# Seven leading pairs, squares through PSUM and decay tables behind the values in a one-core encoder block

## The chip, the core and the metric

The kernel runs on one core of one Trainium2 chip, in one launch. The metric is the device time of that launch in microseconds. Three runs of the kernel before gave 1798.32, 1795.58 and 1797.25 us, median 1797.25.

## What is computed

One layer on 1024 tokens of width 1024, with 16 meta tokens put ahead, all in float32. The mixer normalises the input and multiplies it by one wide weight (`proj = u @ w_in`). The columns of the product feed two branches and their gates:

```python
rq, rk, rv, rg, a_cq, a_ckv, a_kr, a_gret, a_gmla = split(u @ w_in)
y_ret = group_norm(forward_retention(rq, rk, rv) + backward_retention(rq, rk, rv))
y_ret = (silu(rg) * y_ret) @ w_ret_out
y_mla = attention(q(rmsnorm(a_cq)), k(rmsnorm(a_ckv)), v(rmsnorm(a_ckv)), rope(a_kr)) @ w_mla_out
h = h + (sigmoid(a_gret) * y_ret + sigmoid(a_gmla) * y_mla) @ w_o
h = h + (silu(u2 @ w_gate) * (u2 @ w_up)) @ w_down          # u2 = rmsnorm(h)
out = rmsnorm(h)                                            # meta rows dropped
```

The retention weighs its scores with powers of one decay per head and direction. The tables of these powers (128 x 128 per head, rows and columns of powers) are made in the kernel from 16 decay values.

## The kernel before, in words

Every float32 product is made of three matmuls on rounded parts: high by high, high by low, low by high. ScalarE casts the high part of a weight (L209, L153) and VectorE subtracts it to get the low part (L210, L154). A pair is two blocks of 128 output columns by two halves of 512 tokens. `seven` (L183) makes a pair with seven block products instead of eight, in the order of `NAMES` (L30): 11, t2, t3, n1, 21, t4, 22. A product is 12 matmuls with 512 columns (four blocks of the inner dimension, three matmuls each). The sums of weight blocks that t2, t3, n1 and 22 need are made by GpSimd (L191 to L193, L207). `seven_out` (L229) runs the products in order and combines them from PSUM on VectorE. `rest_out` (L300) runs only five products and takes the sum of "11" and "21" from a tile that was kept.

The kernel is written with tile pools. A planner with a time model orders the instructions of each engine: at each moment it takes the ready instruction that comes first in the program. Each engine then works its list in that order, so an instruction that waits holds back all that is behind it. Loads and stores are all issued by SyncE, in its own list.

Order of the mixer's first part:

1. Six pairs (`NP` = 6, L40: the four of `rg` and the first two of the gates) lead with the products "11" and "21" while the input is still being loaded (L345 to L394). Their copies are kept in the pool `hold` (L322), those of the gates in memory (`e_d`). Meanwhile VectorE and ScalarE build the seven input blocks (`second`, L364, and L408 to L418).
2. The rests of the four `rg` pairs (L419, L577, L579), and between them `squares` (L448): the input is loaded again, ScalarE squares each of 16 pieces, and GpSimd adds 14 of them up (L456).
3. Four pairs of values, `project_v` (L525). Each result is transposed on TensorE and copied by ScalarE (L534). After the first come `input_norm` (L458) and `decays` (L479), which makes all decay tables; after the others `finish_gates` (L513), six tiles each: load, scale, Silu or Sigmoid, store.
4. Rotary queries and keys (`project_rope`).
5. Retention, head by head (`core`, L620). Behind each head but the second stands a filler (L805 to L816), a projection that TensorE can do while the retention's long chain of small steps runs: the remaining gates (`project_gates`, seven products, and `rest_gates`, five), `project_q`, `project_key`, `project_kv`. The last two fillers, `project_kv` and a gate pair, stand between the first steps of `z_split` (L825), which splits the retention's result for the next product.
6. The retention's output product (`ret_out`), then attention, the output product and the FFN.

`latent_part` (L710) adds up squares of the latent columns, on GpSimd (L719).

Of the kernel before, what the change touches and what calls it, by code (L numbers as in the profile page):

```python
# [36 lines left out]

DQ, DG, DL = 3, 3, 4

NP = 6  # L40

O_AT = ((6, 1), (6, 2), (6, 3), (7, 0), (7, 1), (7, 2))

# [5 lines left out]
def build(nc, tc, A, out):  # L49
# [4 lines left out]
    def mk(pl, shape, tag, dt=F32):  # L54
        count[0] += 1
        name = f"{tag}_{count[0]}"
        n = int(np.prod(shape[1:]))
        if n % LINE == 0:
            return pl.tile(list(shape), dt, tag=tag, name=name)
        t = pl.tile([shape[0], -(-n // LINE) * LINE], dt, tag=tag, name=name)[:, :n]  # L60
        return t if len(shape) == 2 else t.rearrange("p (a b) -> p a b", b=shape[2])
# [4 lines left out]
    def sb(ctx, name, bufs=1, side=None, space=None):  # L66
        kw = {"reuse_waits": "tile"}
        if side:
            kw["side"] = side
        if space is not None:  # L70
            kw["space"] = space
            if space == DRAM:
                kw = {"space": space}
        return ctx.enter_context(tc.tile_pool(name=name, bufs=bufs, **kw))
# [73 lines left out]
    def slot(pl, dt=F32):  # L148
        return mk(pl, (P, 512), "slot", dt)
# [102 lines left out]
    with ExitStack() as c1:  # L252
# [65 lines left out]

        U = [{} for _ in range(4)]
        cc, a1 = ExitStack(), ExitStack()  # L320
        tb = sb(cc, "tables")
        hold = sb(a1, "hold", NP - 1)  # L322
        with ExitStack() as c2:
            xp, wf, wb = sb(c2, "x", 16), sb(c2, "wfirst", 2), sb(c2, "wfirst_r", 3)
# [108 lines left out]
            dve.tensor_add(t, ps[0:NM, lo : lo + n], t)  # L433
            return t

        dec = mk(tb, (P, 2 * H), "dec")
        kwf, kwb, kwm, gch = [mk(tb, (P, H), t) for t in ("kwf", "kwb", "kwm", "gch")]
        rt = sb(a1, "rope")
        cosf, sinf = mk(rt, (P, S), "cosf"), mk(rt, (P, S), "sinf")
        tm = mk(rt, (NM, 2, 64), "tm")  # L440
# [7 lines left out]
        def squares(c):  # L448
            for k in range(KT):
                t = slot(xl)  # L450
                load(t, A["xT"][k, :, c * 512 : c * 512 + 512])
                if k == 0:
                    act.square(ss[c], t)
                else:
                    act.square(t, t)
                    pool.tensor_add(ss[c], ss[c], t)  # L456

        def input_norm():  # L458
            t = slot(xl)[:, : KT * NM]
# [15 lines left out]
            for c in range(2):  # L475
                for t in (cosf, sinf):
                    dve.tensor_mul(t[:, c * 512 : c * 512 + 512], t[:, c * 512 : c * 512 + 512], rstd_b[:, c * 512 : c * 512 + 512])

        def decays():  # L479
            idx = slot(xl)  # L480
            load(idx, A["idx"][:, : 4 * P])
            idc = mk(rt, (P, 3), "idc")
            load(idc, A["idx"][:, 4 * P :])
            load(dec, A["dec"].broadcast_to([P, 2 * H]))
            act.activation(dec, dec, AF.Exp)
            dve.tensor_scalar(dec, dec, -1.0, None, ALU.mult)
            ip, im = idx[:, 0:P], idx[:, P : 2 * P]
            rowf, rowb = idx[:, 2 * P : 3 * P], idx[:, 3 * P : 4 * P]
            dts = [slot(xl) for _ in range(2)]
            for h in range(H):  # L490
                lf, lb = dec[:, h : h + 1], dec[:, H + h : H + h + 1]
                t = dts[h // 4][:, (h % 4) * P : (h % 4) * P + P]
                dve.tensor_scalar(t, ip, lf, None, ALU.mult)
                dve.scalar_tensor_tensor(t, im, lb, t, ALU.mult, ALU.add)
                act.activation(t, t, AF.Exp)
                store(t_d[h], t)
            tts = [slot(xl), slot(sr)]
            for h in range(H):
                hs = slice((h % 2) * 64, (h % 2) * 64 + 64)
                for t, row, o in ((tts[0], rowf, 0), (tts[1], rowb, H)):  # L500
                    c = slice((h // 2) * P, (h // 2) * P + P)
                    act.activation(t[hs, c], row[hs], AF.Exp, scale=dec[hs, o + h : o + h + 1])
            for p in range(4):
                for i in range(2):
                    store(t_d[8 + 4 * i + p], tts[i][:, p * P : p * P + P])
            for t, i, o, n in ((kwf, 0, 0, P), (kwb, 1, H, P), (kwm, 2, 0, NM)):
                dve.tensor_scalar(t[:n], dec[:n, o : o + H], idc[:n, i : i + 1], None, ALU.mult)
                act.activation(t[:n], t[:n], AF.Exp)
            act.activation(gch[0:64], dec[0:64, 0:H], AF.Exp, scale=float(P))
            act.activation(gch[64:128], dec[64:128, H : 2 * H], AF.Exp, scale=float(P))  # L510
# [11 lines left out]
        unfinished += [(g_d, 2 * j, "11", AF.Sigmoid) for j in range(NP - 4)]  # L522


        def project_v(j):  # L525
            ps = mk(pc, (P, 512), "mm")

            def post(name, t):
                g = side_copy(name, t)
                pt = mk(pc, (P, 512), "mm")  # L530
                for i in range(4):
                    pe.transpose(pt[:, i * P : i * P + P], g[:, i * P : i * P + P], ident)
                vv = slot(cr)
                act.copy(vv, pt)  # L534
                store(v_d[2 * j + int(name[0]) - 1, :, half(name)], vv)

            seven_out(seven(w7, win(4 + j), U, (ps, M1 | M2)), cr, post)
            t = meta_sum(ps, 0, 256)
            for h in range(2):
                store(vm_d[2 * j + h], t[:, h * P : h * P + P])  # L540
# [40 lines left out]
        for j in range(4):  # L581
            project_v(j)
            if j == 0:
                input_norm()
                decays()
            else:
                finish_gates(unfinished[6 * j - 6 : 6 * j])
        for j in range(2):
            project_rope(j, False)
            project_rope(j, True)  # L590
# [119 lines left out]
        def latent_part(t, c, dst, col, first):  # L710
            n = c.stop - c.start
            hi = slot(cr, F32R)[:, :n]
            act.mul(hi, t, col)
            if first:
                act.square(lss[:, c], t)
            else:
                q = slot(cr)[:, :n]
                act.square(q, t)
                pool.tensor_add(lss[:, c], lss[:, c], q)  # L719
            lo = slot(cr)[:, :n]  # L720
            dve.scalar_tensor_tensor(lo, t, col, f(hi), ALU.mult, ALU.subtract)
            store(dst[0][:, c], f(hi))
            store(dst[1][:, c], lo)
# [73 lines left out]
        def project_gates(i):  # L797
            seven_out(seven(w7, win(12 + i), U), cr, gate_post(g_d if i < 4 else s_d, 2 * (i % 4)))

        def rest_gates(i):  # L800
            e = slot(cr)
            load(e, e_d[i])
            rest_out([(seven(w7, win(12 + i), U), e, gate_post(g_d, 2 * i))], cr)

        gates = [lambda i=i: project_gates(i) for i in range(2, 8)]  # L805
        rests = [lambda i=i: rest_gates(i) for i in range(2)]
        fillers = gates[:4] + [rests[0], project_q, rests[1], gates[4], project_key, project_kv, gates[5]]
        for p in range(4):
            t = core_pair(p)
            for h in range(2):  # L810
# [111 lines left out]
    with ExitStack() as c1:  # L922
# [2 lines left out]
        vt = mk(vp, (P, NB + 1, H, P), "vt", F32R)  # L925
        pool.memset(f(vt)[0:48, NB], 0.0)
        ps_s = sb(c1, "ps_s", NS, space=PSUM)
        ps_t = sb(c1, "ps_t", NT, space=PSUM)
        ps_o = sb(c1, "ps_o", NO, space=PSUM)

        w2 = sb(c1, "att2", 2)
        w4 = sb(c1, "att4", 4)
# [510 lines left out]
```

## Time and profile before

| | |
|---|---|
| profiled execution | 1798.07 us |
| its span, first to last instruction | 1796.0 us |
| TensorE busy | 1720.9 us (96%) |
| VectorE busy | 1337.8 us (74%) |
| ScalarE busy | 855.0 us (48%) |
| GpSimd busy | 832.5 us (46%) |
| mean granted TensorE clock | 0.989 |
| memory traffic | 250 MB, mean 139 GB/s |

TensorE is busy nearly all the time, so what counts is where it is idle and where its clock is granted at half. Matmuls overlap, so the durations that the timeline gives for one are longer than the distance to the next; the distance is read from how many start in a stretch.

### The profile page before, as it was taken

The page shows a single profiled execution, that of the slowest core. Times are in us where ns is not written, and L with a number is a line of the kernel's source. Part 1 is how long each engine was busy: PE and PEld are TensorE (multiplying, and loading weights), DVE is VectorE, ACT ScalarE, POOL GpSimd, SP SyncE. Part 2 cuts the span into 40 slices and gives each one's busy share as a digit, 9 for nine tenths or more (in the row PEclk, how much of TensorE's full clock was granted, in tenths as well). Part 3 has the DMA queues.
Part 4 walks back from the last instruction along what each step waited for, and adds up shares of the span by engine and source line. Part 5 has one row for each costly group of instructions (what it writes and reads, how often), then busy time and mean ns, then how long its engine had stood idle before and what let it go on. Part 6 is the DMA issues. An engine that isn't in the chain of part 4 may idle for free.

```text
span 1796.0 us, 26421 instructions
## 1 busy us (share of the span) xinstructions
PE 1720.9 (96%) x8804; PEld 1439.7 (80%) x8804; DVE 1337.8 (74%) x2411; ACT 855.0 (48%) x1606; POOL 832.5 (46%) x654
## 2 busy tenths in 40 slices
PE   8889999999998898999999999899999999999997
PEld 6668777888887777899998888788888888777787
DVE  8755478887988857788879657866667666887966
ACT  7435466344424523678778345423233323543435
POOL 2722257676644421134232423666667666433422
PEclk9999999999999999999999999999999999999999
DMA  7745423556646785011112645233333333754422
GB/s 247 224 142 205 140 92 107 187 179 209 224 141 220 221 291 182 22 37 28 41 46 69 230 159 172 76 106 101 119 98 99 98 115 103 256 185 140 148 61 94
DMA packets 144570, 252.03 MB, mean 140 GB/s; under 512 B 18793, under 2 KB 36642, under 8 KB 144434
## 3 DMA queue, kind: packets, MB, share of 16 engines
q1 hardware_dynamic: 144434, 250.35, 42.6%
q8 instruction: 69, 1.13, 0.3%
q14 instruction: 67, 0.55, 0.1%
HBM read 173.89 MB, written 76.33 MB: 139 GB/s over the span
## 4 chain that ended last, share of the span: by engine, by line
PE 52%; DVE 5%; DMA 3%; ACT 2%; issue 2%; POOL 0%; SPq 0%; DVEq 0%; ACTq 0%; POOLq 0%
PE mm L217 29%; PE mm L137 3%; PE mm L138 3%; PE mm L139 3%; PE o L1027 3%; PE t L997 3%; DVE slot L154 1%; PE s L137 1%; PE s L138 1%; PE s L139 1%; DMA slot<-g_d 1%; DVE slot L210 1%; DMA slot<-f_d 1%; ACT pth L999 1%; PE o L137 1%
## 5 line engine op out<-in xcount | busy, mean ns | idle before, releaser
L217 PE MATMUL mm<-slot,slot 128*128 128x512 f32 x2604 | 596.1, 390 | 9.1 <-DVE slot L210 4.5
L217 PEld LDWEIGHTS mm<-slot,slot 128*128 128x128 f32 x2604 | 488.5, 188 | 115.5 <-DVE slot L210 7.5
L209 ACT CAST slot<-slot 128x512 fp32r<-128x512 f32 (+1 forms) x415 | 247.1, 598 | 464.4 <-PE mm L217 392.2
L210 DVE TENSOR_TENSOR slot<-slot,slot 128x512 fp32r<-128x512 f32 (+1 forms) x415 | 371.9, 897 | 90.4 <-ACT slot L209 81.4
L217 PE MATMUL mm<-ht,slot 128*128 128x512 f32 x648 | 219.7, 400 | 5.9 <-DVE slot L210 2.8
L217 PE MATMUL mm<-h,slot 128*128 128x512 f32 x552 | 190.9, 406 | 13.9 <-ACT slot L209 10.3
L191 POOL TENSOR_TENSOR slot<-slot,slot 128x512 f32<-128x512 f32 (+1 forms) x61 | 88.5, 1451 | 201.9 <-DMA slot<-in_w_u 48.3
L207 POOL TENSOR_TENSOR slot<-slot,slot 128x512 f32<-128x512 f32 (+1 forms) x61 | 87.9, 1442 | 182.2 <-DVE slot L210 170.1
L217 PEld LDWEIGHTS mm<-ht,slot 128*128 128x128 f32 x648 | 122.0, 190 | 34.5 <-ACT slot L209 5.0
L217 PEld LDWEIGHTS mm<-h,slot 128*128 128x128 f32 x552 | 104.3, 191 | 40.6 <-ACT slot L209 12.6
L154 DVE TENSOR_TENSOR slot<-slot,slot 128x512 fp32r<-128x512 f32 x135 | 117.0, 882 | 17.8 <-ACT slot L153 17.0
L217 PE MATMUL mm<-lt,slot 128*128 128x512 f32 x324 | 128.0, 395 | 0.0
L192 POOL TENSOR_TENSOR slot<-slot,slot 128x512 f32<-128x512 f32 (+1 forms) x61 | 83.4, 1367 | 76.0 <-DVE slot L210 70.7
L153 ACT CAST slot<-slot 128x512 fp32r<-128x512 f32 x135 | 82.1, 620 | 71.4 <-DMA slot<-f_d 27.2
L217 PE MATMUL mm<-l,slot 128*128 128x512 f32 x276 | 110.4, 400 | 0.0
L987 DVE TENSOR_SCALAR_CACHE_REDUCE pr<-s,sq_c 128x384 f32<-128x384 f32 (+1 forms) x192 | 103.2, 574 | 6.8 <-PE t L1005 5.4
L139 PE MATMUL mm<-slot,slot 128*128 128x512 f32 (+1 forms) x288 | 105.4, 366 | 0.0
L138 PE MATMUL mm<-slot,slot 128*128 128x512 f32 (+1 forms) x288 | 105.3, 366 | 0.0
L137 PE MATMUL mm<-slot,slot 128*128 128x512 f32 (+1 forms) x288 | 105.2, 367 | 0.0
L1000 DVE TENSOR_TENSOR ptl<-t,pth 128x512 fp32r<-128x512 f32 x128 | 85.8, 685 | 21.4 <-ACT pth L999 20.5
L193 POOL TENSOR_TENSOR slot<-slot,slot 128x512 f32<-128x512 f32 (+1 forms) x61 | 89.2, 1462 | 1.6
L999 ACT CAST pth<-t 128x512 fp32r<-128x512 f32 x128 | 71.9, 580 | 27.1 <-PE t L997 26.7
(360 smaller groups left out, 3460.1 us busy)
## 6 DMA issues: line engine op xcount, KB each, us to landing
slot<-in_w_in SPq DMA_DIRECT2D x104, 256.0 KB
f_d<-slot SPq DMA_DIRECT2D x71, 256.0 KB
slot<-f_d SPq DMA_DIRECT2D x71, 256.0 KB
slot<-in_xT SPq DMA_DIRECT2D x48, 256.0 KB
slot<-z_d SPq DMA_DIRECT2D x44, 256.0 KB
slot<-in_w_g SPq DMA_DIRECT2D x44, 256.0 KB
slot<-in_w_u SPq DMA_DIRECT2D x44, 256.0 KB
slot<-in_w_dq SPq DMA_DIRECT2D x48, 192.0 KB
```

Source lines behind the costliest of these rows:

```text
L137: pe.matmul(ps, sh, mh, start=start, stop=False)
L138: pe.matmul(ps, sh, ml, start=False, stop=False)
L139: pe.matmul(ps, sl, mh, start=False, stop=stop)
L154: dve.tensor_sub(lo, t, f(hi))
L191: pool.tensor_add(s1, a21, a22)
L193: pool.tensor_sub(a21, a21, a11)
L207: pool.tensor_sub(s2, s2, a12)
L209: act.copy(hi, side[b])
L210: dve.tensor_sub(low, side[b], f(hi))
L217: pe.matmul(ps, sw[:, ks], sx, start=begins and q == qs[0] and i == 0, stop=q == nq - 1 and i == 2, skip_group_check=True)
L987: dve.tensor_scalar(pr[:, c], ps[:, :n], sq_c[:, qb : qb + 1], None, ALU.mult, ALU.max, accum_out=mx[:, j : j + 1])
L999: act.copy(pt[0][d], tp)
```

## The change

`NP` goes from 6 to 7: a third gate pair (block 14 of `w_in`) leads with "11" and "21", and in the fillers it is a `rest_gates` of five products where it was a `project_gates` of seven. `hold` has six slots instead of five, `e_d` three pieces instead of two. The small decay tiles move from a pool of their own to `mf`. A square of the input goes to a PSUM tile, and VectorE adds it to the sum; the latent squares are added by VectorE too. `decays` is cut in three (the 128 x 128 tables, the rows, the columns), issued after the first, second and third values, and held on VectorE and ScalarE behind the last copy of those values. That copy is halved between VectorE and ScalarE. The gates are finished in strides of three instead of blocks of six (7, 6 and 6 tiles). The fillers have another order, with the new rest last. In the attention stage the pools of PSUM tiles `ps_o` and `ps_t` are opened in the other order.

```diff
-NP = 6
+NP = 7
...
-        tb = sb(cc, "tables")
...
-        dec = mk(tb, (P, 2 * H), "dec")
-        kwf, kwb, kwm, gch = [mk(tb, (P, H), t) for t in ("kwf", "kwb", "kwm", "gch")]
+        dec = mk(mf, (P, 2 * H), "dec")
+        kwf, kwb, kwm, gch = [mk(mf, (P, H), t) for t in ("kwf", "kwb", "kwm", "gch")]
...
-                    act.square(t, t)
-                    pool.tensor_add(ss[c], ss[c], t)
+                    sq = mk(pc, (P, 512), "mm")
+                    act.square(sq, t)
+                    dve.tensor_add(ss[c], sq, ss[c])
...
+        idx, idc = slot(xl), mk(rt, (P, 3), "idc")
+
         def decays():
-            idx = slot(xl)
             load(idx, A["idx"][:, : 4 * P])
-            idc = mk(rt, (P, 3), "idc")
...
+
+        def decay_rows():
+            rowf, rowb = idx[:, 2 * P : 3 * P], idx[:, 3 * P : 4 * P]
             tts = [slot(xl), slot(sr)]
...
+
+        def decay_columns():
             for t, i, o, n in ((kwf, 0, 0, P), (kwb, 1, H, P), (kwm, 2, 0, NM)):
...
-                act.copy(vv, pt)
+                ends.append((dve.tensor_scalar(vv[:, 0:256], pt[:, 0:256], 1.0, None, ALU.mult), act.copy(vv[:, 256:512], pt[:, 256:512])))
...
             if j == 0:
                 input_norm()
-                decays()
-            else:
-                finish_gates(unfinished[6 * j - 6 : 6 * j])
+            if j < 3:
+                with tc.issue_after(ends[-1][0].ins), tc.issue_after(ends[-1][1].ins):
+                    (decays, decay_rows, decay_columns)[j]()
+            if j:
+                finish_gates(unfinished[j - 1 :: 3])
...
-                pool.tensor_add(lss[:, c], lss[:, c], q)
+                dve.tensor_add(lss[:, c], lss[:, c], q)
...
-        gates = [lambda i=i: project_gates(i) for i in range(2, 8)]
-        rests = [lambda i=i: rest_gates(i) for i in range(2)]
-        fillers = gates[:4] + [rests[0], project_q, rests[1], gates[4], project_key, project_kv, gates[5]]
+        gates = [lambda i=i: project_gates(i) for i in range(NP - 4, 8)]
+        rests = [lambda i=i: rest_gates(i) for i in range(NP - 4)]
+        fillers = [gates[0], gates[1], gates[2], rests[0], project_q, gates[3], gates[4], rests[1], project_key, project_kv, rests[2]]
...
         ps_s = sb(c1, "ps_s", NS, space=PSUM)
+        ps_o = sb(c1, "ps_o", NO, space=PSUM)
         ps_t = sb(c1, "ps_t", NT, space=PSUM)
-        ps_o = sb(c1, "ps_o", NO, space=PSUM)
```

## Rows read from the trace of the kernel before

**Rows 1.** 50 us stretches: us; PE, PEld, DVE, ACT, POOL busy (instructions); clock; DMA; GB/s.

```profile
0.00:50.00 50.00, 39.05 (x153) 30.15 (x154) 41.66 (x57) 35.40 (x64) 14.38 (x22) 0.98 0.71 244
50.00:100.00 50.00, 39.40 (x158) 30.34 (x157) 34.95 (x55) 25.88 (x59) 35.30 (x23) 0.91 0.64 204
...
150.00:200.00 50.00, 49.02 (x277) 39.60 (x276) 32.44 (x48) 27.97 (x49) 11.91 (x8) 1.00 0.67 232
...
1300.00:1350.00 50.00, 50.00 (x223) 41.40 (x222) 34.56 (x42) 16.77 (x29) 34.34 (x24) 1.00 0.33 106
```

**Rows 2.** TensorE's timeline to 130 us: start, duration, instruction, idle before, its releaser.

```profile
43.60 0.50 PE L217 MATMUL mm<-ht,slot 128*128 128x512 f32 x1 [1.35 <-ACT slot L209]
...
47.20 0.50 PE L217 MATMUL mm<-hn,slot 128*128 128x512 f32 x1 [2.35 <-ACT slot L209]
...
48.87 1.22 PE L217 MATMUL mm<-ht,slot 128*128 128x512 f32 x2 [0.93 <-DVE slot L210]
...
75.44 0.73 PE L217 MATMUL mm<-h,slot 128*128 128x512 f32 x2 [0.67 <-DVE slot L210]
...
79.25 0.50 PE L217 MATMUL mm<-ht,slot 128*128 128x512 f32 x1 [1.25 <-ACT slot L209]
...
96.65 0.79 PE L217 MATMUL mm<-h,slot 128*128 128x512 f32 x1 [8.67 <-ACT slot L209]
```

**Rows 3.** The same columns as rows 1, in stretches of 5 us.

```profile
10.00:15.00 5.00, 5.00 (x21) 4.06 (x21) 3.63 (x6) 3.14 (x5) 0.00 (x0) 1.00 1.06 399
...
45.00:50.00 5.00, 1.87 (x5) 1.24 (x6) 5.00 (x10) 2.63 (x6) 1.11 (x1) 0.83 0.68 223
50.00:55.00 5.00, 5.00 (x20) 4.02 (x19) 4.83 (x9) 0.89 (x3) 5.00 (x2) 0.83 0.02 5
...
75.00:80.00 5.00, 3.31 (x13) 2.12 (x13) 1.76 (x4) 2.57 (x5) 2.81 (x3) 1.00 0.94 313
...
95.00:100.00 5.00, 3.35 (x9) 2.68 (x10) 2.78 (x5) 2.99 (x10) 1.28 (x1) 0.55 0.63 186
```

**Rows 4.** VectorE's timeline, 30 to 100 us.

```profile
31.24 0.68 DVE L154 TENSOR_TENSOR slot<-slot,slot 128x512 fp32r<-128x512 f32 x1
...
83.36 1.58 DVE L210 TENSOR_TENSOR slot<-slot,slot 128x512 fp32r<-128x512 f32 x1
86.11 5.37 DVE L493 TENSOR_SCALAR slot<-slot,dec 128x128 f32<-128x128 f32 x6 [1.17 <-POOL slot L191]
...
92.84 0.68 DVE L302 TENSOR_TENSOR slot<-mm,slot 128x512 f32<-128x512 f32 x1
93.44 1.12 DVE L494 SCALAR_TENSOR_TENSOR slot<-slot,dec,slot 128x128 f32<-128x128 f32 x4
```

**Rows 5.** ScalarE's timeline, 70 to 100 us.

```profile
77.36 1.33 ACT L455 ACTIVATE slot<-slot 128x512 f32<-128x512 f32 x2 [2.84 <-DMA slot<-in_xT]
...
86.01 3.32 ACT L502 ACTIVATE slot<-slot,dec 64x128 f32<-64x128 f32 x8 [3.07 <-DMA slot<-in_idx]
...
93.49 2.07 ACT L502 ACTIVATE slot<-slot,dec 64x128 f32<-64x128 f32 x5
```

**Rows 6.** Line 456, GpSimd's adds of squares: shortest, median, longest (ns), first and last start.

```profile
L456 POOL TENSOR_TENSOR ss<-ss,slot x14: 1257/1300/1970, 62.8 to 89.9; 128x512 f32<-128x512 f32 x14
```

**Rows 7.** Line 451, the loads for the squares: who waited for them (us, times).

```profile
  ACT ss L453: 6.3, 2
  ACT slot L455: 4.3, 4
```

**Rows 8.** TensorE's waits over the whole span: us in total, times, longest.

```profile
PE mm L160 <- POOL lss L719: 2.4, 2, 2.1
```

**Rows 9.** ScalarE's timeline behind the first values: a table load and what follows.

```profile
147.91 1.28 ACT L469 ACT_TABLE_LOAD   x1
149.20 0.40 ACT L469 ACTIVATE rst<-mm,eps 128x8 f32<-128x8 f32 x2
```

**Rows 10.** Columns of rows 1, 5 us in which the last gate pair runs.

```profile
605.00:610.00 5.00, 5.00 (x24) 4.13 (x24) 5.00 (x5) 3.14 (x6) 4.31 (x4) 1.00 0.91 283
```

More of the change, by code (lines that the diff above doesn't have):

```diff
@@ L487, in decays @@
             ip, im = idx[:, 0:P], idx[:, P : 2 * P]
-            rowf, rowb = idx[:, 2 * P : 3 * P], idx[:, 3 * P : 4 * P]
             dts = [slot(xl) for _ in range(2)]
@@ L522, in build @@
         unfinished += [(g_d, 2 * j, "11", AF.Sigmoid) for j in range(NP - 4)]
+        ends = []
         def project_v(j):
```

## The prediction

> **What bounds the kernel now.** I read the busy shares first, then TensorE's busy time in stretches of 50 us, then its timeline wherever a stretch fell short. TensorE is the bound: in a full stretch some 222 matmuls with 512 columns start, one each 50 / 222 = 0.225 us [rows 1]; a product of 12 is 2.7 us. The first two stretches fall short, with 153 and 158 [rows 1]. In them I see two idle places that the change touches.
>
> Place A, 42 to 49 us. The leading products end, and TensorE waits 1.35, 2.35 and 0.93 us, in all 4.6, for the high and low parts of the rests' weights [rows 2]. VectorE is busy without a break there, building input blocks [rows 3]. The granted clock is 0.83 in each of the two stretches from 45 to 55 us [rows 3]: 1.7 us of each at the lower level, 1.2 GHz. TensorE was busy in some 2.8 of these 3.4 us and lost nearly half of them, 1.3 us.
>
> Place B, 75 to 100 us. Waits of 0.67, 1.25 and 8.67 us, in all 10.6 [rows 2]. The long one is work in the wrong order. ScalarE waits 3.07 us for the table `idx` and works off eight exponentials of the decay rows before it casts the next weight, and more of them later [rows 5]. VectorE has the decay products ahead of its subtractions. Six of them take 5.37 us, 0.9 each, while GpSimd adds squares until about 91 us [rows 4, 6]; a little later four of their like take 1.12 us, 0.28 each [rows 4]. Then the clock is 0.55 in 95 to 100 us, with 3.35 us of busy time [rows 3], nearly all of it at 1.2 GHz: 1.4 us lost. B is 12.0 us in all.
>
> **The change, part by part.**
>
> *Seventh pair.* 24 matmuls (5.4 us) go from the last gate filler to the lead, ahead of place A. The lead also gets two casts and two copies on ScalarE, two loads and two stores of 256 KB on SyncE's list, and two subtractions of 0.68 us on VectorE [rows 4], 1.4 us. VectorE is the late engine at A, so the state that TensorE reached at 48.87 us comes 1.4 us later, with 5.4 us more work done: of 4.6 us idle 4.6 + 1.4 - 5.4 = 0.6 remain. I take 1.2, since the loads join a DMA that is full at the start, 1.06 [rows 3]. After the waits of 0.67 and 1.25 us at B the clock was still 1.00 [rows 3], so I let it stay there: 1.3 us more. Gain 3.4 + 1.3 = 4.7 us. Bounds: 0 (VectorE falls behind by as much as the work added) and 5.9 (all of A).
>
> What is late next is the other end. The filler beside the splits of the retention's result has 5.4 us less. VectorE is full there, 5.00 of 5 us [rows 10], and loses only three operations of 0.68 us, 2.0. If VectorE sets the pace, 5.4 - 2.0 = 3.4 us come back as idle time; if the splits needed first are early enough, none. I take the middle, 1.7. The other fillers change places, but as many stand ahead of `project_kv` as before; their order I cost at nothing, 1 us either way, since the retention's chain is covered by whichever filler is at hand.
>
> *Squares through PSUM.* 14 adds of 1.3 us leave GpSimd [rows 6] and become adds of 0.68 us on VectorE (the add with one PSUM operand, L302 [rows 4]), 9.5 us over some 30. In return VectorE's subtractions, 1.58 us beside GpSimd's adds and 0.68 elsewhere [rows 4], lose that delay; ten of them at 0.6 to 0.9 are 6 to 9 us. VectorE comes out about even, and GpSimd is free for the weight sums. A wait is added: the add waits for the square, the square for its input tile, and behind the add stand subtractions that TensorE needs. ScalarE already waited 6.3 + 4.3 us for that input [rows 7], `idx` now keeps one of six load slots meanwhile, and the waits of 0.67 and 1.25 us at B are of this stretch. I leave these 1.9 us standing.
>
> *Decays in three parts.* The long wait of B loses its cause, since the decay work is held behind the first values: 8.67 + 1.4 = 10.1 us gained. The work itself comes later: 16 VectorE operations at 0.28 us [rows 4], 4.5 us, behind the first values; 16 exponentials at 3.32 / 8 = 0.41 us [rows 5], 6.6 us on ScalarE, behind the second. Its 16 table stores of 64 KB wait on SyncE's list for these, with weight loads behind them, where the DMA is 0.67 busy [rows 1]. VectorE is busy 32 of 50 us there and ScalarE 28 [rows 1], and up to three split weights lie ready, so a burst costs TensorE what goes beyond two products, 5.4 us: about 1 us. Exponentials now stand between Silu and Sigmoid, and each third of the gates has one Sigmoid, so I count ten table loads in place of three; a load takes 1.28 us and the next operation starts 0.01 us after it [rows 9]. Seven more are 9.0 us of ScalarE's free 22. I take 1.5 us for all of this; bounds 0 and 4.5 + 6.6 + 9.0 = 20.1.
>
> The Trainium skill, "ScalarE: Activation LUTs", section "What ACT_TABLE_LOAD costs", puts a switch at 1.28 us for the load and 1.38 us for a drain. By it seven switches would be 18.6 us, an estimate from that page; the trace has the load and no drain, so the measured row decides.
>
> *The rest.* The halved copy of the values may take longer in sum, but TensorE waits for that copy nowhere: nothing, at most 1 us. The latent adds leave a GpSimd for which TensorE waited 2.4 us [rows 8]; VectorE is busy at the same place, so I take 0.5 of it, bounds 0 and 2.4. The order of the PSUM pools and the place of the small tiles: nothing, 1 us either way, since as many tiles are there as before.
>
> *Sum.* -4.7 + 1.7 - 10.1 + 1.5 - 0.5 = -12.1 us. The profiled execution took 1798.07 us, 0.8 above the median of the three runs, and becomes 1786.0; against the median it is 1797.25 - 12.1 = 1785.2. I forecast 1785.
>
> **The rivals.**
>
> *The seventh pair only moves its idle time.* The whole 5.4 us come back beside the splits. For it: VectorE full in rows 10. Against: the split that is made last is needed last. Time: 1785.2 - 1.7 + 5.4 = 1789.
>
> *The decay bursts hit TensorE behind the values.* For it: the wait of 8.67 us shows what bursts on two engines do. Against: no squares run beside them then, and `idx` is long loaded. With half of the 20.1 us: 1785.2 - 1.5 + 10.0 = 1794.
>
> *Squares and adds in lockstep (slower).* One rest holds three of the four banks of the PSUM pool that the squares use, so a square may find one bank: ScalarE waits for VectorE's add to free it, VectorE for the square. 14 rounds of 0.66 (half of 1.33 [rows 5]) and 0.68 us are 18.8 us in which neither makes weights. For it: the waits of rows 7 would now hold both engines. Against: the rest holds its banks for some five products only, 13.5 us. If all 18.8 us fall on TensorE, 1785.2 + 18.8 = 1804; it is slower than before, beyond what can be told, from 15.6 us on.
>
> *All idle goes.* A, B and the latent wait vanish and nothing comes back: 5.9 + 12.0 + 2.4 = 20.3 us, 1777.
>
> **How the numbers follow.** Forecast 0.62, with a range of its own from 1779 to 1791. Idle moved 0.12. Decay bursts 0.13. Lockstep 0.08. All gone 0.05. The measurement tells 0.2%, 3.6 us, from no change: faster is below 1793.7, slower above 1800.8. Faster gets 0.62 + 0.12 + 0.05, and 0.05 of the bursts: 0.84. Same gets 0.08 of the bursts and 0.01 of the lockstep: 0.09. Slower 0.07. The range from 1777 to 1796 leaves out the lockstep and the worst bursts, about 0.12, and little below.
>
> **What would show it.** Right: the lead runs to about 47.5 us, TensorE idles under 2 us behind it, and the clock stays 1.00; no wait over 2 us between 60 and 110 us; the decay operations start behind the first values' last copy; GpSimd is busy some 20 us less; the last rest is followed by up to 2 us of idle time. Wrong: VectorE waiting for squares with TensorE idle; waits over 2 us behind the first or second values; a long wait at the start of `ret_out`; or changes of several us from attention on, where I expect none.

## The result, and the profile after

| | before | after |
|---|---|---|
| median (lowest to highest) | 1797.14 us (1793.35 to 1800.51), 6 runs | 1787.72 us (1783.00 to 1790.65), 6 runs |
| profiled execution | 1798.07 us | 1783.00 us |
| its span | 1796.0 us | 1781.2 us |
| busy: TensorE, VectorE, ScalarE, GpSimd | 1720.9, 1337.8, 855.0, 832.5 us | 1718.1, 1346.5, 861.8, 798.4 us |
| mean granted clock | 0.989 | 0.989 |

The ratio is 0.9944, 95% interval 0.9924 to 0.9963: 9.4 us faster at the medians, where 12 were forecast. A second set of six runs, beside other runs of the kernel before, gave 0.9939 (0.9919 to 0.9958). Two of the runs reported below took 2435.76 and 2840.85 us, at granted clocks of 0.652 and 0.556, and every median, ratio and interval leaves them out. The profiled execution is the fastest of its six. A second trace of the same kernel, which I call the repeat, has a span of 1790.2 us, so two traces of one kernel can lie 9 us apart; I compare traces only from landmark to landmark. Idle time of TensorE in the first trace is 1781.2 - 1718.1 = 63.1 us, before it was 75.1.

The answer to [rows 1] and [rows 3], the kernel after: stretches with their length, then busy time (instructions) of PE, PEld, DVE, ACT, POOL, then clock, DMA share, GB/s.

```profile
0.00:50.00 50.00, 39.46 (x157) 31.22 (x158) 41.54 (x55) 35.47 (x61) 10.95 (x21) 0.97 0.70 245
50.00:100.00 50.00, 49.98 (x220) 41.01 (x219) 37.90 (x59) 21.96 (x40) 17.46 (x12) 1.00 0.70 235
45.00:50.00 5.00, 3.40 (x9) 2.68 (x10) 5.00 (x8) 1.06 (x2) 0.40 (x1) 0.70 0.37 130
550.00:600.00 50.00, 40.77 (x190) 33.66 (x190) 39.46 (x70) 29.41 (x56) 17.18 (x11) 0.83 0.75 240
```

Place B is gone: 220 matmuls in 50 to 100 us where there were 158, at full clock. Place A is not: the first 50 us have 157 where there were 153, and from 45 to 50 us the clock is 0.70. What stands at A now, from TensorE's timeline (start, duration, instruction, idle time before it and what ended it), the answer to [rows 2]; the last three lines are what is new further on:

```profile
46.60 0.92 PE L341 MATMUL mm<-h,slot 128*128 128x512 f32 x2 [4.35 <-DVE slot L154]
...
586.44 0.21 PE L160 MATMUL mm<-ones,lss 128*16 128x1 f32 x2 [3.07 <-DVE lss L727]
589.35 0.76 PE L217 MATMUL mm<-ht,slot 128*128 128x512 f32 x1 [2.69 <-DVE skv_c L741]
...
692.85 0.98 PE L137 MATMUL s<-k,q 96*128 96x384 f32 x2 [5.87 <-DMA q<-qr]
```

The three waits of place A became one of 4.35 us, inside the lead. The lead has fourteen weights. The last but one was cast on ScalarE at 37.76 us, the last at 40.84; their low parts are the lines at 45.87 and 48.88 in VectorE's timeline of the same kernel, behind four block operations that GpSimd's sums (41 to 45 us, the second fence, GpSimd's timeline) stretch:

```profile
37.13 0.68 DVE L154 TENSOR_TENSOR slot<-slot,slot 128x512 fp32r<-128x512 f32 x1
37.73 2.49 DVE L411 TENSOR_TENSOR lt<-slot,ht 128x512 fp32r<-128x512 f32 x4
40.14 5.81 DVE L414 SCALAR_TENSOR_TENSOR slot<-slot,cols,slot 128x512 f32<-128x512 f32 x4
45.87 0.68 DVE L154 TENSOR_TENSOR slot<-slot,slot 128x512 fp32r<-128x512 f32 x1
...
48.88 0.68 DVE L154 TENSOR_TENSOR slot<-slot,slot 128x512 fp32r<-128x512 f32 x1
```

```profile
40.75 1.29 POOL L191 TENSOR_TENSOR slot<-slot,slot 128x512 f32<-128x512 f32 x1 [12.35 <-DMA slot<-in_w_in]
42.12 1.60 POOL L192 TENSOR_TENSOR slot<-slot,slot 128x512 f32<-128x512 f32 x1
43.67 1.72 POOL L193 TENSOR_TENSOR slot<-slot,slot 128x512 f32<-128x512 f32 x1
```

The squares, the answer to [rows 6], by VectorE now: one line's instructions with the shortest, median and longest duration in ns, first and last start. Below it, from the groups of ScalarE's instructions between 130 and 250 us (busy us, mean ns), the largest group of table loads; with three single ones there are 10, as counted.

```profile
L456 DVE TENSOR_TENSOR ss<-mm,ss x14: 680/685/692, 63.9 to 80.9; 128x512 f32<-128x512 f32 x14
```

```profile
L522 ACT ACT_TABLE_LOAD x7 | 9.0, 1283 | 2.3 <-issue 1.4 <-DVE slot L521 0.8
```

Two landmarks measure everything that follows. Both are waits that every kernel here has: one of 0.9 us in the rotary projections (H) and one of 2.25 us at an output product of the first attention head (O). After:

```profile
257.28 0.73 PE L217 MATMUL mm<-ht,slot 128*128 128x512 f32 x2 [0.94 <-DVE slot L210]
...
723.92 0.39 PE L1035 MATMUL o<-pth,vt 128*128 128x256 f32 x1 [2.25 <-ACT pth L1007]
```

Before, H is at 266.47 and O at 737.27 us. After is 9.2 us ahead at H, with 5.4 us more work done by then, and 13.4 ahead at O. In the repeat O is at 728.07, 9.2 ahead, which is what the medians show.

### The profile page after: what moved, and what is told of

The parts are those of the page before. It is cut to its first block, busy times and chain, and to the rows that moved or that the text cites. A ratio compares the mean times of both kernels' runs of the same rounds, so it can differ in the third digit from the quotient of the medians.

```text
span 1781.2 us, 26455 instructions
## 1 busy us (share of the span) xinstructions
PE 1718.1 (96%) x8804; PEld 1440.9 (81%) x8804; DVE 1346.5 (76%) x2448; ACT 861.8 (48%) x1614; POOL 798.4 (45%) x633
## 4 chain that ended last, share of the span: by engine, by line
PE 53%; DVE 7%; DMA 3%; issue 2%; ACT 2%; SPq 0%; POOL 0%; DVEq 0%; ACTq 0%; POOLq 0%
PE mm L217 33%; PE o L1035 3%; PE mm L137 3%; PE mm L138 3%; PE mm L139 3%; PE t L1005 3%; DVE slot L154 1%; PE s L137 1%; PE s L138 1%; PE s L139 1%; DMA slot<-g_d 1%; DVE ptl L1008 1%; DVE slot L210 1%; DVE pr L995 1%; PE o L138 1%
## 5 line engine op out<-in xcount | busy, mean ns | idle before, releaser
L217 PE MATMUL mm<-h,slot 128*128 128x512 f32 x536 | 184.5, 403 | 0.0
L154 DVE TENSOR_TENSOR slot<-slot,slot 128x512 fp32r<-128x512 f32 x137 | 116.2, 862 | 17.9 <-ACT slot L153 17.2
L217 PE MATMUL mm<-l,slot 128*128 128x512 f32 x268 | 106.6, 398 | 0.0
```

The lines of the kernel that those rows point to most:

```text
L154: dve.tensor_sub(lo, t, f(hi))
L217: pe.matmul(ps, sw[:, ks], sx, start=begins and q == qs[0] and i == 0, stop=q == nq - 1 and i == 2, skip_group_check=True)
```

## The experiments

Every kernel was timed beside runs of the kernel before. "Matmuls" are those that its trace counts from 0 to 40 us and from 40 to 100 us; one or two that are under way at 40 us count in both.

| kernel | matmuls | H | O | median, us | ratio to before (95%) |
|---|---|---|---|---|---|
| before | 135, 175 | 266.47 | 737.27 | 1797.14 | |
| after | 140, 237 | 257.28 | 723.92 | 1787.72 | 0.9944 (0.9924 to 0.9963) |
| after, repeat | 136, 235 | 258.31 | 728.07 | 1788.74 | 0.9939 (0.9919 to 0.9958) |
| six pairs | 133, 228 | 254.29 | 722.90 | 1785.28 | 0.9928 (0.9915 to 0.9942) |
| squares on GpSimd | 133, 237 | 259.83 | 727.19 | 1788.09 | 0.9942 (0.9929 to 0.9955) |
| decays not held | 131, 225 | 262.29 | 730.84 | 1790.04 | 0.9951 (0.9939 to 0.9964) |
| both of these | 136, 194 | 267.74 | 736.69 | 1799.77 | 1.0008 (0.9996 to 1.0019) |
| PSUM pools as before | 138, 236 | 258.12 | 724.44 | 1786.71 | 0.9936 (0.9921 to 0.9950) |
| last blocks free | 122, 251 | 258.86 | 727.05 | 1792.31 | 0.9960 (0.9943 to 0.9976) |
| the same, six pairs | 128, 242 | 252.65 | 722.81 | 1785.63 | 0.9926 (0.9909 to 0.9943) |
| low part ahead of blocks | 134, 239 | 257.84 | 725.50 | 1789.95 | 0.9952 (0.9935 to 0.9968) |
| whole gate last | 135, 235 | 258.65 | 735.20 | 1796.68 | 0.9985 (0.9969 to 1.0001) |
| rests' sums on VectorE | 143, 247 | 254.23 | 722.86 | 1786.48 | 0.9934 (0.9916 to 0.9952) |
| the last three together | 140, 250 | 255.13 | 731.35 | 1794.97 | 0.9976 (0.9965 to 0.9986) |

**Second trace of the change.**

> The changed kernel once more, for a second trace and more times beside the others. At 40 us the traces so far have begun between 131 and 140 wide matmuls (140 in the changed kernel), so up to 2 us of a difference between two traces is the start. If that is so: ratio to the kernel before 0.994 to 0.9955, the wait of 4.3 us inside the lead again, no wait over 0.5 us from 51 to 190 us, and 131 to 140 matmuls at 40 us.

It came out so: 136 matmuls by 40 us, the wait of 4.38 us inside the lead, no wait over 0.5 us from 51 to 190 us. In the kernels whose edits act only behind the lead, TensorE, VectorE and ScalarE begin with the same instructions in the same order, and still their counts at 40 us go from 131 to 140; the difference is there by 20 us, while ScalarE waits for the first loads of the input. So up to 9 matmuls, 2 us, of a difference between traces is how soon the first loads arrived.

**Six pairs.**

```diff
-NP = 7
+NP = 6
-fillers = [..., project_key, project_kv, rests[2]]
+fillers = [..., project_key, project_kv, gates[5]]
```

> The changed kernel with six pairs in the lead again; the seventh pair's matmuls are the last gate filler beside the retention. Theory (the seventh pair's low parts queue behind VectorE's block building, so the idle moves into the lead and only about 1 us is won): 1.0 to 2.5 us over the changed kernel, ratio to the kernel before 0.995 to 0.996; the waits of 1.35, 2.35 and 0.93 us behind the lead are back, the wait of 4.35 us inside it is gone. Rival (the sum as predicted: 4.7 us won at the lead, 1.7 lost beside the splits): 3 us over, ratio 0.9965. Rival (the pair's order also filled the retention's stage): 5 us or more over, ratio 0.998, with waits between 590 and 705 us.

All three expectations were on the wrong side: it is not slower. The waits of A are back. TensorE's timeline of this kernel:

```profile
44.01 0.50 PE L217 MATMUL mm<-ht,slot 128*128 128x512 f32 x1 [1.29 <-ACT slot L209]
47.61 0.80 PE L217 MATMUL mm<-hn,slot 128*128 128x512 f32 x1 [2.35 <-ACT slot L209]
49.27 1.22 PE L217 MATMUL mm<-ht,slot 128*128 128x512 f32 x2 [0.44 <-DVE slot L210]
...
580.75 0.21 PE L160 MATMUL mm<-ones,lss 128*16 128x1 f32 x2 [2.07 <-DVE lss L727]
...
690.68 0.76 PE L137 MATMUL s<-k,q 96*128 96x384 f32 x2 [4.08 <-DMA q<-qr]
```

At H seven pairs are 3.0 us (repeat 4.0) later with 5.4 us more work done, a gain of 2.4 (1.4); of that 7 (3) matmuls at 0.225 us, 1.6 (0.7), were already there by 40 us. What is left is 0.8 and 0.7 us. From H to O six pairs take 722.90 - 254.29 = 468.6 us, seven 466.6 (repeat 469.8): of the 5.4 us less work, 2.0 us or nothing are saved and 3.4 to 6.6 come back as idle time. With a whole gate behind it the wait of 2.69 us for `skv_c` is absent. So by the traces the pair loses 2.6 to 5.9 us, and the times point the same way: the mean of the runs stands 13.4 us under the mean of the kernel before with six pairs, 10.1 and 10.1 in the two sets with seven. These 3.3 us alone are within the noise of six runs each.

**Squares back on GpSimd, decays not held, and both.**

```diff
-                    sq = mk(pc, (P, 512), "mm")
-                    act.square(sq, t)
-                    dve.tensor_add(ss[c], sq, ss[c])
+                    act.square(t, t)
+                    pool.tensor_add(ss[c], ss[c], t)
```

```diff
-            if j < 3:
-                with tc.issue_after(ends[-1][0].ins), tc.issue_after(ends[-1][1].ins):
-                    (decays, decay_rows, decay_columns)[j]()
+                decays()
+                decay_rows()
+                decay_columns()
```

> The changed kernel with the squares of the input and their sums on ScalarE and GpSimd as before. Theory (the decays held behind the values removed the long wait; the squares' way through PSUM removed only the small ones): the waits of 0.7 and 1.3 us at 75 to 80 us are back and nothing else, 2 us over the changed kernel, ratio to the kernel before 0.9955. Rival (GpSimd's adds, which slow VectorE's subtractions from 0.68 to 1.58 us, were the cause of the long wait): 6 to 10 us over, ratio 0.998 to 1.0, with waits of several us between 80 and 100 us.

> The changed kernel with the three parts of the decay tables in one place, not held behind the values; squares through PSUM stay. Theory (the order held the weights back): VectorE's decay products take 0.28 us in place of 0.9 beside an idle GpSimd, which gives back 3.7 of the 8.7 us; the rest of the long wait, 5 us, and some 1 us of clock are back between 85 and 100 us, 4.5 us over the changed kernel after the bursts behind the values (1.5) are gone, ratio to the kernel before 0.997. Rival (the squares on GpSimd were the whole cause): no wait over 1 us at 75 to 110 us, the same time as the changed kernel or 1.5 us less, ratio 0.9935 to 0.9945.

> The changed kernel with both undone: the decay tables in one place and not held, the squares on ScalarE and GpSimd. Theory (the two make the long wait together: the decay work ahead of the weights, stretched by GpSimd's adds; either one alone brings 0 to 3 us of it back): waits of 8 to 12 us in all are back between 75 and 110 us, 8 to 11 us over the changed kernel, ratio to the kernel before 0.999 to 1.0005. Rival (the two add up): 3 to 4 us over, waits of 2 to 3 us in all, ratio 0.996. Rival (other parts of the change removed the wait): no wait over 1 us there beyond the one of 1.8 us, ratio 0.995.

Each alone costs little: with the squares back on GpSimd no time, and no wait over 0.5 us from 51 to 190 us; with the decays free 1 to 2 us in the times, which is within their noise, and 2.9 us at H, with one wait of 1.78 us at 93.06 where 5 were expected. Both together cost 11.5 us (1.0008 against 0.9944) and bring most of B back: waits of 1.51 and 5.37 us, 6.9 where 8 to 12 were expected and B had 10.6, and 174 matmuls in the stretch below, against 220 after and 158 before. The stretch from 50 to 100 us, columns as above, with squares on GpSimd, with free decays, with both:

```profile
50.00:100.00 50.00, 49.96 (x216) 40.81 (x215) 32.69 (x46) 21.68 (x39) 35.26 (x24) 0.98 0.71 230
```

```profile
50.00:100.00 50.00, 48.22 (x204) 39.20 (x204) 41.28 (x78) 29.52 (x68) 14.28 (x10) 0.96 0.81 260
```

```profile
50.00:100.00 50.00, 43.12 (x174) 34.37 (x173) 37.58 (x59) 29.36 (x66) 32.15 (x23) 0.92 0.70 222
```

TensorE's longest wait of that stretch in the kernel with both, and what VectorE (second fence) and GpSimd (third) do ahead of it:

```profile
94.47 1.22 PE L217 MATMUL mm<-ht,slot 128*128 128x512 f32 x2 [5.37 <-DVE slot L210]
```

```profile
88.32 2.55 DVE L491 TENSOR_SCALAR slot<-slot,dec 128x128 f32<-128x128 f32 x2
90.79 1.36 DVE L492 SCALAR_TENSOR_TENSOR slot<-slot,dec,slot 128x128 f32<-128x128 f32 x1
92.08 1.48 DVE L491 TENSOR_SCALAR slot<-slot,dec 128x128 f32<-128x128 f32 x2
93.48 0.34 DVE L492 SCALAR_TENSOR_TENSOR slot<-slot,dec,slot 128x128 f32<-128x128 f32 x1
93.74 0.68 DVE L210 TENSOR_TENSOR slot<-slot,slot 128x512 fp32r<-128x512 f32 x1
```

```profile
88.28 1.28 POOL L191 TENSOR_TENSOR slot<-slot,slot 128x512 f32<-128x512 f32 x1 [2.80 <-DVE slot L314]
89.52 1.26 POOL L455 TENSOR_TENSOR ss<-ss,slot 128x512 f32<-128x512 f32 x1
90.74 1.26 POOL L193 TENSOR_TENSOR slot<-slot,slot 128x512 f32<-128x512 f32 x1
91.96 1.31 POOL L455 TENSOR_TENSOR ss<-ss,slot 128x512 f32<-128x512 f32 x1
```

The low part that TensorE needs stands behind decay products that last up to 1.36 us each beside GpSimd, where they take 0.28 and 0.33 us in the kernel after. So the long wait needed both: decay work ahead of the weights, and GpSimd's adds to stretch it.

**PSUM pools in the old order.**

```diff
-        ps_o = sb(c1, "ps_o", NO, space=PSUM)
         ps_t = sb(c1, "ps_t", NT, space=PSUM)
+        ps_o = sb(c1, "ps_o", NO, space=PSUM)
```

> The changed kernel with the PSUM pools of the attention in the order of before (transposes' banks ahead of the outputs'). As predicted: nothing, within 1 us. Theory from the trace of the changed kernel (the attention's transposes lie on banks that come free early, so the first heads run among the last retention outputs, and a wait of about 6 us for a load of q stands behind them): the first heads' transposes move from 675 to about 690 us, the waits among the retention's outputs are back, 3 to 5 us, and the wait for q with its half clock shrinks by as much or more; in all 4 us less to 3 us more than the changed kernel, ratio to the kernel before 0.992 to 0.996. If the earlier heads are pure gain: 4 to 5 us over, ratio 0.997.

The work moves, the time does not. What the expectation calls transposes are the key products of the first heads, which write into the transposes' pool (`t<-ckh,kh`). They start at 672.97 us after; in this kernel they come 16 us later and wait (second line), and the wait for `q` at 692.85 us is gone. O is at 724.44, 0.5 us later, all of it there already at H.

```profile
676.32 0.50 PE L217 MATMUL mm<-h,slot 128*128 128x512 f32 x1 [1.69 <-ACT slot L233]
688.67 0.44 PE L137 MATMUL t<-ckh,kh 128*128 128x384 f32 x1 [3.89 <-DVE slot L242]
```

**The order of VectorE's work in the lead.** Three kernels. In the first the blocks t4 and 22 are no longer held behind the t3 blocks but written behind the adds of t2; the planner then put them earlier, from 23.46 us on, and not later, so its edit did not do what the expectation says. The second is the same with six pairs. In the third the hold stays, with the lead's last low part in front:

```diff
-            with tc.issue_after(made[0].ins), tc.issue_after(made[1].ins):
-                for q in range(4):                      # t4, 22
+            def last_blocks():
+                for q in range(4):                      # t4, 22
...
+            rest_out(..., last_blocks)                  # called behind the t2 adds
```

```diff
-            with tc.issue_after(made[0].ins), tc.issue_after(made[1].ins):   # t4, 22
+            with tc.issue_after(lows[0].ins), tc.issue_after(made[1].ins):   # lows[0]: last low part of the lead
```

> The changed kernel with VectorE's last eight block inputs (t4 and 22) built behind the adds of the rests' t2 products, not behind the first two weights' parts. Theory (the seventh pair's low part waits 4.35 us behind four block operations of 1.45 us): the wait of 4.35 us inside the lead and its half clock go, the lead runs through to about 47 us; no wait over 1.5 us behind it; 4 to 5.5 us under the changed kernel, ratio to the kernel before 0.9915 to 0.992. Rival (VectorE is full in that stretch, so the blocks delay whatever stands behind them): waits of 3 to 5 us at the rests' t4 and 22 products, same time as the changed kernel, ratio 0.9945.

> As the kernel with the blocks built late, but with six pairs in the lead. With seven pairs the lead covers VectorE's blocks, with six it has 5.4 us less to cover them. Theory (with the blocks out of the way the seventh pair still gives back 3.4 us beside the splits, so it is worth 2 us at most): 0 to 2 us over the seven pairs with late blocks, ratio to the kernel before 0.992 to 0.993. Rival (late blocks make the lead late by all that the pair had covered): 4 to 5 us over, ratio 0.9945, with waits of 4 us or more at 42 to 50 us.

> The changed kernel with VectorE's last eight block inputs (t4 and 22) held behind the seventh pair's last low part. Theory A (that low part is only queued wrongly: its cast was ready at 41.5 us and it ran at 45.87): the wait of 4.35 us inside the lead goes, 1 to 2 us of it come back ahead of the rests, the clock stays up; 2.5 to 4 us under the changed kernel, ratio to the kernel before 0.992 to 0.993. Theory B (VectorE has more work from 24 to 52 us than TensorE has, in whatever order, as in the kernel with the blocks left free, which ended even): a wait of 3 to 5 us stands behind the lead in place of the one inside it, ratio 0.994 to 0.996.

With the blocks free the wait inside the lead goes from 4.35 to 2.44 us, at 33 us. With the low part first it goes altogether. (The cast that the expectation has ready at 41.5 us is the last; its low part ran at 48.88, and 45.87 is that of the weight before.) VectorE's and TensorE's timelines of that kernel (lines stand two lower in its text, L156 for L154, L416 for L414):

```profile
38.01 1.28 DVE L156 TENSOR_TENSOR slot<-slot,slot 128x512 fp32r<-128x512 f32 x2
...
41.63 0.68 DVE L156 TENSOR_TENSOR slot<-slot,slot 128x512 fp32r<-128x512 f32 x1
42.23 5.85 DVE L416 SCALAR_TENSOR_TENSOR slot<-slot,cols,slot 128x512 f32<-128x512 f32 x4
```

```profile
49.62 0.50 PE L219 MATMUL mm<-hn,slot 128*128 128x512 f32 x1 [0.73 <-ACT slot L211]
51.75 0.74 PE L219 MATMUL mm<-ht,slot 128*128 128x512 f32 x2 [1.40 <-DVE slot L212]
70.30 0.47 PE L219 MATMUL mm<-ht,slot 128*128 128x512 f32 x1 [1.65 <-ACT mm L457]
```

The waits behind the lead, 0.73 and 1.40 us, are those of theory A, and the order did win: TensorE's matmuls from 40 to 65 us and from 65 to 75 us (the columns of [rows 1]), of the change and of this kernel:

```profile
40.00:65.00 25.00, 20.63 (x83) 16.02 (x82) 21.24 (x30) 12.03 (x23) 10.95 (x7) 0.93 0.62 209
65.00:75.00 10.00, 10.00 (x46) 8.29 (x45) 9.69 (x17) 6.84 (x14) 1.38 (x2) 1.00 0.84 289
```

```profile
40.00:65.00 25.00, 22.87 (x93) 18.10 (x92) 21.42 (x29) 9.25 (x19) 13.14 (x7) 0.93 0.59 189
65.00:75.00 10.00, 8.35 (x38) 6.61 (x37) 9.12 (x15) 8.32 (x15) 1.30 (x1) 1.00 0.96 332
```

The repeat has 81 and 46. So by 65 us the order has won 10 to 12 matmuls, 2.3 to 2.7 us. Eight are lost again by 75 us, around the wait of 1.65 us at 70.30, which neither theory has. Its releaser is a square of the input on its way through PSUM, and VectorE's combining add, queued behind two adds of squares, ends within 0.05 us of it; which of the two held TensorE is open. With six pairs the same wait stands at 67.34 us with 1.24 us. At H, less the difference by 40 us, 0.8 to 0.9 us are left, and the time, 0.9952, is theory B's. So VectorE's order in the lead does matter, and what it wins is given back behind it.

With the blocks free, six pairs beat seven when timed together, 1785.63 against 1792.31 us, and their intervals only touch, at 0.9943: the pair costs some 6 us there.

**The first rests' weight sums on VectorE.**

```diff
-    def seven(pools, srcs, blocks, meta=None):
+    def seven(pools, srcs, blocks, meta=None, sums=pool):
-        pool.tensor_add(s1, a21, a22)
+        sums.tensor_add(s1, a21, a22)
...
-            rest_out([(seven(w7, win(0), U), es[0], rg_post(0)),
+            rest_out([(seven(w7, win(0), U, None, dve), es[0], rg_post(0)),
```

> The changed kernel with the four weight sums of each of the two first rests on VectorE and not on GpSimd. Theory (VectorE's operations take 1.45 to 1.79 us beside GpSimd's sums and 0.68 to 0.74 without, some 6 us in all between 23 and 46 us, and the eight sums cost VectorE 0.68 each, 5.4 us): the block operations take 0.74 us each, VectorE ends about where it did; the wait inside the lead shrinks from 4.35 to about 1 us, and 2 to 4 us stand behind the lead, since the sums now come behind the blocks; within 1.5 us of the changed kernel, ratio 0.993 to 0.9955. Rival (the long durations are something else than GpSimd): block operations of 1.45 us stay, 5 us over, ratio 0.997.

The four block operations took 2.73 us instead of 5.81, VectorE had ten instructions more from 10 to 52 us in the same busy time (39.5 us after 39.4), and TensorE's wait fell to 2.29 us. No wait over 0.5 us stands behind the lead, where 2 to 4 were expected. The order changed too: the last but one low part now comes ahead of the blocks. VectorE's and TensorE's timelines of this kernel:

```profile
37.20 0.69 DVE L154 TENSOR_TENSOR slot<-slot,slot 128x512 fp32r<-128x512 f32 x1
...
39.61 2.73 DVE L414 SCALAR_TENSOR_TENSOR slot<-slot,cols,slot 128x512 f32<-128x512 f32 x4
```

```profile
46.01 0.73 PE L341 MATMUL mm<-h,slot 128*128 128x512 f32 x2 [2.29 <-DVE slot L154]
```

It is the only one of these that kept what it won at A: from 40 to 65 us it counts 93 matmuls, as many as with the low part first, then no wait follows; from 40 to 100 us it has 10 and 12 more than the change and the repeat, and H is 3 to 4 us earlier, of which 0.7 to 1.6 were there by 40 us. What of this is the order and what the sums, this kernel does not separate. At O 1 us (repeat 5 us) is left, and the time, 0.9934, is not told apart from the change.

**A whole gate as the last filler, and all three.**

```diff
-fillers = [..., project_q, gates[3], gates[4], rests[1], project_key, project_kv, rests[2]]
+fillers = [..., project_q, gates[3], rests[1], rests[2], project_key, project_kv, gates[4]]
```

> The changed kernel with another order of the fillers: a whole gate product (5.4 us more than a rest) stands last, beside the splits of the retention's result, and a rest takes its place beside the retention. Theory (the 3.4 us that come back are the waits of 3.07 and 2.69 us at 586 to 590 us and their half clock, which stand there because the last filler is short): these waits shrink to about 2 us as in the kernel with six pairs, the mean clock of 550 to 600 us rises from 0.83 to about 0.90; 2 to 3.5 us under the changed kernel, ratio to the kernel before 0.992 to 0.993. Rival (the short filler is missed where it now stands, beside the retention): new waits of 2 to 5 us between 300 and 550 us, ratio 0.994 or above.

> The last three together: last blocks behind the seventh pair's low part, a whole gate as last filler, the first rests' weight sums on VectorE. If the effects add up as the theories have them (3, 3 and 0): 5 to 7 us under the changed kernel, ratio to the kernel before 0.9905 to 0.992. If VectorE sets the end of the lead whatever its order: only the filler counts, 2 to 3.5 us under, ratio 0.992 to 0.993. If neither: 0.994 or above.

The rival's place was right and its price too low: 7 to 8 us lost (0.9985 against 0.9944 and 0.9939). The gate was missed at the last heads of the retention, and of the waits beside the splits, 7.6 us after (1.87, 3.07 and 2.69), 5.3 stayed (3.13 and 2.15). TensorE's timeline:

```profile
531.33 0.74 PE L217 MATMUL mm<-h,slot 128*128 128x512 f32 x2 [1.00 <-DVE slot L210]
540.40 1.66 PE L690 MATMUL mm<-ident,slot 128*128 128x128 f32 x5 [4.46 <-DVE slot L687]
559.69 0.34 PE L222 MATMUL mm<-slot,um 128*48 128x128 f32 x1 [3.93 <-ACT slot L209]
...
588.91 0.28 PE L776 MATMUL mm<-ident,slot 16*128 16x16 f32 x1 [3.13 <-DVE slot L729]
```

All three together (0.9976) carry the same loss. Their lead has no wait inside, one of 3.47 us behind it at 50.09, and no more matmuls by 100 us than the sums alone.

## Why the prediction was right in its sum, and where it was not

The sum was -12.1 us, the runs say -9.4. Two terms missed, on opposite sides: the seventh pair by some 6 us, decays and squares by up to 3. That the sum came this close is in part luck.

- **Decays and squares.** The sum had -10.1 for B and +1.5 for the bursts, -8.6. The kernel with both undone, which keeps the other parts, stands at 1.0008, and the change at 0.9944: these two parts are worth 11.5 us, more than the whole gain (against the repeat, timed together, 11.3 with an interval of 2.4 either way; 9.4 at H). The mechanism, decay work ahead of the weights and stretched by GpSimd, was right. But the sum gave all of the 10.1 to the hold and nothing to the squares, and either of them in place keeps the long wait away: with the squares moved, the hold is worth 1 to 3 us. The 1.9 us left standing went as well. The bursts cost nothing that can be found: against the repeat the free decays lack 10 matmuls from 40 to 100 us (2.3 us), and at H, less 5 matmuls by 40 us (1.1 us), they are 2.9 us behind, so nothing was saved behind the values. Ten table loads came as counted.

  The Trainium skill, "ScalarE: Activation LUTs", section "What ACT_TABLE_LOAD costs", adds a drain of 1.38 us to each load. The trace again shows none: a load starts at 140.01 us, lasts 1.28, and the next exponential starts at 141.30.

- **The failed step: "of 4.6 us idle 4.6 + 1.4 - 5.4 = 0.6 remain".** It took VectorE to be 1.4 us later for two subtractions, with its order else unchanged. The low parts of the lead's last two weights were queued behind four block operations, and a wait of 4.35 us stands in the lead, with the clock at 0.70 from 45 to 50 us. In place of 4.7 us the pair won about 0.7 at H. With the low part ahead of the blocks 2.3 to 2.7 us come back by 65 us, so the order cost that much; the waits of 0.73 and 1.40 us behind that lead remain, and VectorE, busy 39.4 of the 42 us from 10 to 52 us, has little room to fill them. How much of the rest is VectorE's load is not shown.

- **Idle time coming back at the end** was sized at 1.7 us with 3.4 as its far end; the traces show 3.4 to 6.6 (two traces of one kernel differ by 3 us there). The pair as a whole was forecast at -3.0 us and measured at some +3. The rival "the seventh pair only moves its idle time" came true at this end; it too kept the 4.7 us at A, which did not come.

- **The fillers' order** was costed at nothing, since the retention is "covered by whichever filler is at hand". One exchange of a gate and a rest cost 7 to 8 us, so that reason is wrong; what the change's own order is worth against the old one was not run.

- **The PSUM pools** at "nothing, 1 us either way" held in the time (0.9936 without), but not for the reason given: the first heads' key products moved by 16 us, and a wait for `q` took the place of others. This is also the shift from attention on that I did not expect.

- **Latent adds, -0.5 us:** not seen. The wait of 2.1 us for GpSimd [rows 8] is now one of 3.07 us for VectorE, 2.07 with six pairs; it was not tried alone.

- **Lockstep of squares and adds** did not appear in the change: 14 adds at 685 ns, no wait at TensorE. The waits of 1.65 and 1.24 us in two of the other kernels are the nearest to it.

The two kernels with six pairs, all else as changed but for the free blocks of one, are 3.1 us faster than the change over 12 runs each (worked out from the means less those of the kernel before; interval about 2.5 either way), so by these runs such a version beats both. Six pairs with the rests' sums on VectorE would be the next to try; it was not run. What makes two traces of one kernel differ by 3 us between H and O stays open.

## To carry to other kernels

Where an idle place is set by an engine that is full there, added work for the idle engine covers little if it also brings work for the full one: count the full engine's microseconds, not the gap, and ask where in its list the new pieces will stand. Two causes can each be enough to remove and both needed to make a wait, so undo them singly and together before giving either the credit. A filler has a price where it is taken away, and it is read from the waits that appear there.

## What the runs showed of the hardware

VectorE operations with two inputs in SBUF are stretched beside GpSimd's adds, and those with one input in PSUM are not. The four block operations of L414 took 1510 ns in the mean beside the sums, up to 1793, and 747 ns without; the adds of L456 kept to 680 to 692 ns throughout, among them the one at 77.41 us, beside a GpSimd sum that began at 77.57. Two tiles in SBUF are not the only case: the decay products of L491, with one tile in SBUF and a column of scalars, took up to 1.3 us beside GpSimd in the kernel with both undone, where their like take 0.28 in the kernel after. So the rests' sums cost VectorE no more time when it made them itself, at 0.69 us each, than when GpSimd made them beside it.

The Trainium skill, "SBUF — State Buffer", section "Who interferes with whom", says that a VectorE instruction with two SBUF inputs contends with a GpSimd instruction that reads SBUF, and one with at most one does not, outside VectorE's two-port modes. The rows of L414 and L456 agree with it. Whether the products of L491 run in such a mode, no run here shows.
